# A mixture of 32 experts in 16 blocks of 128 slots and one for the overflow, or in 13 blocks ordered by token counts

## The chip, the core and the metric

One core of a Trainium2 chip runs the whole program. The metric is the device time of one execution in microseconds; the kernel before was run three times.

## The reference

Two transformer-like blocks run one after the other on 512 tokens of 1024 numbers, in float32. Only the expert layer that ends the first block changes:

```python
g_prob = softmax(t @ w_rg + b_rg)            # one of 4 groups
e_prob = softmax(e_logits of that group)     # top 2 of its 8 experts
for every expert e of 32:
    hid = silu(t @ w_gate[e]) * (t @ w_up[e]) * combine[:, e]
    y += hid @ w_down[e]                      # 1024 -> 256 -> 1024
```

So there are 1024 pairs of a token and an expert, and each expert has three matrices of 1024 x 256 floats, 100.7 MB in all, that come from HBM once per execution.

## The kernel before

A router stage gives each token its two experts, their weights (`Wc`) and its place in each expert's queue (`rank`). Each expert has `CAP` = 64 places. Two experts share a block of 128 slots, two blocks make a round of the loop at L1253, and there are eight rounds. For a round, `onehot` (L1055) builds tables token x slot: `ph` with ones, and `pw` with the combining weights, made on POOL (L1070). `gather_piece` (L1074) multiplies the tokens, kept as a high part `gh` and a low part `gl`, with `ph`, and so puts the round's 256 slots in columns (`xg`).

For a block, gate-up (L1270) multiplies the slots with the gate and up weights `we` of its two experts, each in 64 of the 128 output rows: one expert occupies columns 0 to 63 of the array, the other 64 to 127. `slots_back` (L1091) transposes the block's `pw` by four products (L1095). `hidden` (L1103) applies silu on ACT and DVE, `hidden_t` (L1110) transposes the result by two products (L1113), ACT copies it (L1116), and the down product (L1293) uses the weights `wd`. Outputs are split into two parts (`eoh`, `eol`, L181 and L184). `combine` (L1129; products L1125 and L1126) adds the slots of the round before into the tokens `x1`, eight chunks of 128 columns. The order on TensorE is written by hand: gate-up, transposes, four chunks of combining, hidden transposes, two gather pieces for the next round, down.

All weights are loaded through SP's queue, in program order. `load_up` (L1035) takes tiles of 512 KB from a ring of eight (`wp`), which a block's gate-up weights fill; `load_down` (L1048) takes halves of 256 KB from another ring of eight (`hp`). The second block's gate-up weights lie in spare buffers. A load waits in SP's queue until the last product that reads its tile is done, and the loads behind it wait with it.

Tokens past the 64th of an expert go to overflow blocks. The first of these, block 0, always runs: its expert's number is read from memory by SP (L1137), its weights are loaded a second time (L1141, L1146), its tokens are gathered at L1167, and its products are L1305 and L1318. Further overflow blocks run in a loop (L1348) as often as needed. The places of the overflow are worked out on DVE (L1200 to L1250). `last_ada` are modulation rows whose transposes (L348) stand in front of the first gate-up; their products (L334) come earlier, in four column groups of 32.

## Time and profile before

| | |
|---|---|
| median of three runs | 1312.29 us |
| runs | 1311.86, 1312.29, 1320.4 us |
| the profiled execution: span from the first to the last instruction | 1319.8 us |
| PE busy, share of the span | 1261.9 us, 96% |
| DVE, ACT, POOL busy | 764.8, 474.7, 274.3 us |
| bytes moved | 208.13 MB, mean 158 GB/s |

The profiled execution's own time is not among the runs by name; its span is 0.6 us below the slowest of them. PE's busy time includes pipelined products that overlap, and a busy PE is not PE at its peak. The expert stage lies between about 453 and 780 us of the span. Timelines give an instruction's start and length; products overlap, so their cost is read from one start to the next.

### The profile page before, as it was taken

Reading aid. Unit: us, or ns where it says so; the run is one execution under the profiler, and the core shown is the slowest. Engines: PE = TensorE matmul, PEld = TensorE weight load, DVE = VectorE, ACT = ScalarE, POOL = GpSimd, SP = SyncE. Lnnn points to the kernel's source line nnn. Section 1 sums busy time; section 2 is a strip of 40 time slices with the busy share of each in tenths; the row PEclk is TensorE's granted clock in tenths of the full one; section 3 lists DMA queues with packets and bytes.
Section 4 is the critical chain, followed back from the end, with each engine's and each line's share of the span. In section 5 each row is a group of like instructions: output and inputs, shape, how many; then the busy total and the mean of one; then the engine's idle time right before and its main releaser. Section 6 shows DMA issues by size and latency. Waiting matters only on the chain. (4 is left out here: it accounts for less than half of the span.)

```text
span 1319.8 us, 18564 instructions
## 1 busy us (share of the span) xinstructions
PE 1261.9 (96%) x6814; PEld 902.2 (68%) x6820; DVE 764.8 (58%) x1616; ACT 474.7 (36%) x1052; POOL 274.3 (21%) x239
## 2 busy tenths in 40 slices
PE   6999999999999799999999999999999999899997
PEld 3676766788887545655565458777777777676676
DVE  6857776544443723232333364477778777677767
ACT  4444445333333322212222223344444444345330
POOL 4243121000010210000000041223333330333321
PEclk9999999999999899999999969999999999989999
DMA  9625334122274468998899813122121122112221
GB/s 356 231 80 178 119 112 176 49 96 96 96 287 138 177 227 333 339 351 327 322 346 351 304 50 116 68 80 81 64 81 48 64 81 80 37 44 80 97 80 64
DMA packets 77341, 208.13 MB, mean 158 GB/s; under 512 B 9344, under 2 KB 9472, under 8 KB 77248
## 3 DMA queue, kind: packets, MB, share of 16 engines
q1 hardware_dynamic: 75264, 200.80, 42.2%
q0 software_dynamic: 1840, 6.03, 1.4%
q8 instruction: 55, 0.90, 0.3%
q14 instruction: 38, 0.31, 0.1%
q10 hardware_dynamic: 144, 0.09, 0.1%
HBM read 204.79 MB, written 2.10 MB: 157 GB/s over the span
## 5 line engine op out<-in xcount | busy, mean ns | idle before, releaser
L200 DVE TENSOR_TENSOR wlo<-w,whi 128x512 fp32r<-128x512 f32 x200 | 157.0, 824 | 114.0 <-ACT whi L199 101.6
L211 PE MATMUL ps_d<-x2h,whi 128*128 128x512 f32 x352 | 143.2, 407 | 0.0
L213 PE MATMUL ps_d<-x2h,wlo 128*128 128x512 f32 x352 | 138.4, 393 | 0.0
L212 PE MATMUL ps_d<-x2l,whi 128*128 128x512 f32 x352 | 138.1, 392 | 0.0
L199 ACT ACTIVATE whi<-w 128x512 fp32r<-128x512 f32 x200 | 115.4, 620 | 37.9 <-PE ps_d L212 16.5
L667 ACT ACTIVATE p<-st,mn 128x128 f32<-128x128 f32 (+3 forms) x128 | 71.0, 556 | 148.2 <-DVE mn L659 148.2
L1270 PE MATMUL ps_o<-we,xg 128*64 128x512 f32 x512 | 112.6, 592 | 0.0
L1270 PEld LDWEIGHTS ps_o<-we,xg 128*64 128x64 f32 x512 | 36.7, 137 | 72.7 <-issue 64.4
L184 DVE TENSOR_TENSOR eol<-ps_sc,eoh 128x512 fp32r<-128x512 f32 x33 | 22.8, 692 | 102.8 <-ACT eoh L181 94.5
L211 PEld LDWEIGHTS ps_d<-x2h,whi 128*128 128x128 f32 x352 | 66.8, 190 | 20.4 <-issue 5.3
L211 PE MATMUL ps_d<-h1h,whi 128*128 128x512 f32 x192 | 78.4, 409 | 0.0
L213 PEld LDWEIGHTS ps_d<-x2h,wlo 128*128 128x128 f32 x352 | 66.5, 189 | 15.3 <-DVE wlo L200 0.6
L212 PEld LDWEIGHTS ps_d<-x2l,whi 128*128 128x128 f32 x352 | 66.9, 190 | 12.5
L213 PE MATMUL ps_d<-h1h,wlo 128*128 128x512 f32 x192 | 75.0, 391 | 0.0
L212 PE MATMUL ps_d<-h1l,whi 128*128 128x512 f32 x192 | 74.9, 390 | 0.0
L1083 PE MATMUL ps_d<-ph,gh 128*128 128x256 f32 x256 | 66.1, 296 | 1.6 <-DVE ph L1062 1.6
L1070 POOL TENSOR_TENSOR pw<-ph,route 128x256 f32<-128x256 f32 x32 | 21.7, 707 | 218.6 <-PE ps_o L1270 199.1
L1084 PE MATMUL ps_d<-ph,gl 128*128 128x256 f32 x256 | 64.5, 290 | 0.0
L692 DVE TENSOR_SCALAR p<-p,rl 128x128 f32<-128x128 f32 (+3 forms) x128 | 58.7, 459 | 4.6
L1293 PE MATMUL ps_sc<-wd,p 128*64 128x512 f32 x256 | 58.5, 598 | 2.1 <-ACT p L1116 2.0
L1083 PEld LDWEIGHTS ps_d<-ph,gh 128*128 128x128 f32 x256 | 51.0, 199 | 2.1 <-ACT gh L939 1.3
L1084 PEld LDWEIGHTS ps_d<-ph,gl 128*128 128x128 f32 x256 | 51.1, 200 | 0.0
(669 smaller groups left out, 2756.5 us busy)
## 6 DMA issues: line engine op xcount, KB each, us to landing
we<-in_w_e_dram SPq DMA_DIRECT2D x124, 512.0 KB, 7.7
w<-in_w_dram SPq DMA_DIRECT2D x68, 512.0 KB, 3.3
wd<-in_w_e_dram SPq DMA_DIRECT2D x132, 256.0 KB, 4.7
wa<-in_w_ada_dram SPq DMA_DIRECT2D x32, 512.0 KB, 5.2
w<-in_w_out_dram SPq DMA_DIRECT2D x32, 512.0 KB, 3.2
wa<-in_w_ada_dram SPq DMA_DIRECT2D x32, 256.0 KB, 5.4
w<-in_v_dram SPq DMA_DIRECT2D x12, 512.0 KB, 7.5
w<-in_w_o_dram SPq DMA_DIRECT2D x8, 512.0 KB, 3.7
```

The costliest lines, as they stand in the source:

```text
L184: (ge if lo_eng == "g" else ve).tensor_tensor(lo, src, hi.bitcast(F32), op=OP.subtract)
L199: se.activation(hi, raw[:, s], AF.Copy)
L200: ve.tensor_tensor(lo, raw[:, s], hi.bitcast(F32), op=OP.subtract)
L211: pe.matmul(o, lh, rh, start=first, stop=False)
L212: pe.matmul(o, lh, rl, start=False, stop=False)
L213: pe.matmul(o, ll, rh, start=False, stop=last)
L667: se.activation(pt[:, :w], u["st"][s][:, :w], AF.Exp, bias=u["mn"][s], scale=-1.0, accum_out=l)
L692: ve.tensor_scalar(u["p"][s][:, :w], u["p"][s][:, :w], rl, None, op0=OP.mult)
L1083: pe.matmul(o[:, q * 256:(q + 1) * 256], gh[g][:, s], r, start=t == 0, stop=False)
L1084: pe.matmul(o[:, q * 256:(q + 1) * 256], gl[g][:, s], r, start=False, stop=t == 3)
L1270: pe.matmul(gu[64 * s:64 * s + 64, :], xg[k // 2][:, c0:c0 + CAP], ws[j, s, k // 2][k % 2], start=k == 0, stop=k == KC - 1, tile_position= ...
L1293: pe.matmul(o[64 * s:64 * s + 64, :], ht[:, kk * P + 64 * s:kk * P + 64 * s + 64], ws[j, s, kk, h], start=kk == 0, stop=kk == 1, tile_posi ...
```

## The change

The 32 experts are put into 13 blocks of four quarters of 32 slots. Experts 0 to 5 keep two quarters each (64 places), in blocks 0 to 2, and their loads need no number from the chip. The other 26 are sorted on the chip by their token counts: the largest gets three quarters (96 places), the next twelve two, the last thirteen one (32). Blocks 3, 6 and 9 hold two experts of 64 places; blocks 4, 5, 7, 8, 10 and 11 hold one of 64 and two of 32; block 12 holds the one of 96 and one of 32. Blocks go in groups of two, the last group of three. Block 0 for the overflow is gone: tokens without a place go to the loop, which starts from its first pass.

The sort: DVE counts for each expert how many have more tokens (`place`) and builds a selecting table `pick` from it and a new constant table, which POOL's queue loads (`rtab`). Two transposes and four small products then give, for each quarter, the places and weights of the tokens (`zkeys`, `zwts`) and its expert's number (`eid`). SP reads these numbers into registers ahead of the loads of block 3 and later ones. A third expert's weights lie in the small rings `tab` and `pt`.

The order on TensorE is new too. Two chunks of combining and a gather piece stand between the quarters of gate-up; two more chunks stand behind the slot transposes; the rest comes behind the hidden transposes. The last block opens three chunks of the final combining ahead of its down product. The modulation transposes and the overflow's arithmetic are moved behind block 0's gate-up.

```diff
+NS = 6
+TILES = [2] * NS + [3] + [2] * 12 + [1] * 13
+GROUPS = ((0, 1), (2, 3), (4, 5), (6, 7), (8, 9), (10, 11, 12))
+def _blocks():
+    two, one = list(range(NS + 1, NS + 13)), list(range(NS + 13, NE))
+    out = [[(2 * i, 2), (2 * i + 1, 2)] for i in range(NS // 2)]
+    for _ in range(3):
+        out.append([(two.pop(0), 2), (two.pop(0), 2)])
+        for _ in range(2):
+            out.append([(two.pop(0), 2), (one.pop(0), 1), (one.pop(0), 1)])
+    out.append([(NS, 3), (one.pop(0), 1)])
+    assert not two and not one
+    return out
+BLOCKS = _blocks()
+ZT = [(p, 32 * i) for b in BLOCKS[2:] for p, n in b for i in range(n)]
+NZ = len(ZT)
...
+    def expert(p):
+        if p < NS:
+            return p
+        z = [q for q, _ in ZT].index(p)
+        return nc.values_load(eid[0:1, z:z + 1], engines=[mybir.EngineType.SP], min_val=0, max_val=NE - 1)
+    def fetch(t, e, i, c=slice(0, 1024)):
+        if isinstance(e, int):
+            nc.sync.dma_start(t, w_e[e, i, :, c])
+        else:
+            nc.sync.dma_start(t, w_e[bass.ds(e, 1), i, :, c].rearrange("o p c -> p (o c)"))
+    def halves(alloc, e, i):
+        t = [alloc() for h in range(2)]
+        for h in range(2):
+            fetch(t[h], e, i, slice(h * 512, (h + 1) * 512))
+        return t
+    regs = {}
+    def load_up(n, spare=False):
+        regs[n] = [expert(p) for p, _ in BLOCKS[n]]
         for i in range(4):
-            for s in range(2):
+            for s, e in enumerate(regs[n]):
                 if spare:
-                    t = [big("we") for h in range(2)]
-                    for h in range(2):
-                        nc.sync.dma_start(t[h], w_e[2 * j + s, i, :, h * 512:(h + 1) * 512])
+                    ws[n, s, i] = halves(lambda: big("we"), e, i)
+                elif s == 2 and i < 2:
+                    ws[n, s, i] = halves(lambda: tmp("tab"), e, i)
                 else:
-                    t = wload(w_e[2 * j + s, i], "we")
-                    t = [t[:, 0:512], t[:, 512:1024]]
-                ws[j, s, i] = t
-    def load_down(j):
-        for h in range(2):
-            for i in range(2):
-                for s in range(2):
-                    t = ws[j, s, i, h] = hp.tile([P, 512], F32, tag="h", name="wd")
-                    nc.sync.dma_start(t, w_e[2 * j + s, 4 + i, :, h * 512:(h + 1) * 512])
+                    t = wp.tile([P, 1024], F32, tag="w", name="we")
+                    fetch(t, e, i)
+                    ws[n, s, i] = [t[:, 0:512], t[:, 512:1024]]
+    def load_down(n):
+        es = regs.pop(n)
+        for ss in ((0, 1), (2,)):
+            for h in range(2):
+                for i in range(2):
+                    for s in ss:
+                        if s < len(es):
+                            t = hp.tile([P, 512], F32, tag="h", name="wd") if s < 2 else tmp("pt")
+                            ws[n, s, 4 + i, h] = t
+                            fetch(t, es[s], 4 + i, slice(h * 512, (h + 1) * 512))
...
         o = bank("d")
-        for q in range(2):
-            d = 2 * c + q
+        w = ph[0].shape[1]
+        n = 512 // w
+        for q in range(n):
+            d = n * c + q
             for t in range(4):
                 g = 2 * t + d // 4
                 s = slice((d % 4) * P, (d % 4 + 1) * P)
-                r = ph[t // 2][:, (t % 2) * 256:(t % 2 + 1) * 256]
-                pe.matmul(o[:, q * 256:(q + 1) * 256], gh[g][:, s], r, start=t == 0, stop=False)
-                pe.matmul(o[:, q * 256:(q + 1) * 256], gl[g][:, s], r, start=False, stop=t == 3)
+                pe.matmul(o[:, q * w:(q + 1) * w], gh[g][:, s], ph[t], start=t == 0, stop=False)
+                pe.matmul(o[:, q * w:(q + 1) * w], gl[g][:, s], ph[t], start=False, stop=t == 3)
         x_ = big("xg")
-        for q in range(2):
-            s = slice(q * 256, (q + 1) * 256)
-            se.activation(x_[:, s], o[:, s], AF.Identity, bias=mods[:, 24 + 2 * c + q:25 + 2 * c + q])
-        xg.append(x_)
+        for q in range(n):
+            s = slice(q * w, (q + 1) * w)
+            se.activation(x_[:, s], o[:, s], AF.Identity, bias=mods[:, 24 + n * c + q:25 + n * c + q])
+            xg.append(x_[:, s])
...
-    def load_block0():
-        er = nc.values_load(eb0[0:1, 0:1], engines=[mybir.EngineType.SP], min_val=0, max_val=NE - 1)
...
+    rtab = big("rtab")
+    ge.dma_start(rtab[:, :288], consts_d[:, 640:928])
+    ph, pw = onehot(rank[:, :, 0:4], Wc[:, :, 0:4], CAP, weights)
...
-    run(last_ada[0][1], last_ada[1][1])
...
+    keyr, keyc, own, place = cv(NE), cv(1), cv(NE), cv(1)
+    ve.scalar_tensor_tensor(keyr, cnt, float(NE), rtab[:, 220:252], op0=OP.mult, op1=OP.add)
+    ve.tensor_tensor(own, keyr, rtab[:, 253:285], op=OP.mult)
+    ve.tensor_reduce(keyc, own, axis=AX.X, op=OP.add)
+    above = cv(NE)
+    ve.tensor_scalar(above, keyr, keyc, None, op0=OP.is_gt)
+    ve.tensor_reduce(place, above, axis=AX.X, op=OP.add)
+    pick = big("pick")
+    ve.tensor_scalar(pick[:, :4 * NZ], rtab[:, :4 * NZ], place, None, op0=OP.is_equal)
...
+    o = bank("tr")
+    pe.transpose(o[:, 0:P], rank1.rearrange("p t e -> p (t e)"), ident)
+    pe.transpose(o[:, P:2 * P], Wc.rearrange("p t e -> p (t e)"), ident)
+    turned = big("turned")
+    ve.tensor_copy(turned[:, :2 * P], o[:, :2 * P])
+    zkeys, zwts = cz(4, NZ), cz(4, NZ)
+    eid = small([P, NZ], "eid", I32, bufs=1)
...
+    def order_out():
+        o = bank("tr")
+        for i in range(2):
+            pe.matmul(o[:, 4 * NZ * i:4 * NZ * (i + 1)], turned[:, i * P:(i + 1) * P], pick[:, :4 * NZ], start=True,
+                      stop=True)
+        pe.matmul(o[:, 8 * NZ:9 * NZ], rtab[:, 252:253].to_broadcast([P, P]), pick[:, :NZ], start=True, stop=True)
+        pe.matmul(o[:, 9 * NZ:9 * NZ + NE], capc[:, 0:1].to_broadcast([P, P]), ident[:, :NE], start=True, stop=True)
+        v = lambda a: a.rearrange("p (t z) -> p t z", t=4)
+        ve.tensor_copy(eid, o[:, 8 * NZ:9 * NZ])
+        ve.tensor_tensor(zkeys, v(o[:, :4 * NZ]), rtab[:, None, 176:176 + NZ].to_broadcast([P, 4, NZ]), op=OP.subtract)
+        ve.tensor_copy(zwts, v(o[:, 4 * NZ:8 * NZ]))
+        ve.tensor_copy(caps, o[:, 9 * NZ:9 * NZ + NE])
+    def spill_in():
...
+    def gate_up(n, b, i, gu, xg):
+        whole = all(c == 2 for _, c in BLOCKS[n])
+        for k in (2 * i, 2 * i + 1):
+            z = 0
+            for s, (_, c) in enumerate(BLOCKS[n]):
+                m = 64 if whole else 32
+                for z in range(z, z + c, m // 32):
+                    a = 32 * z
+                    pe.matmul(gu[a:a + m, :], xg[k][:, b * P + a:b * P + a + m], ws[n, s, i][k % 2], start=k == 0,
+                              stop=k == KC - 1, tile_position=(0, a))
+                z += m // 32
...
     prev = None
-    for q in range(NQ):
-        if q + 1 < NQ:
-            ph, pw_next = onehot(q + 1)
+    opened = []
+    for gi, group in enumerate(GROUPS):
+        nxt = GROUPS[gi + 1] if gi + 1 < len(GROUPS) else ()
         xg_next, outs, pts = [], [], []
-        for b in range(2):
-            j = 2 * q + b
-            if j + 2 < NE // 2:
-                if j:
-                    load_up(j + 2)
-                load_down(j + 2)
-            elif q == NQ - 1 and b == 0:
-                w0 = load_block0()
-                po0, pw0 = onehot0()
+        nb = len(group)
+        gathers = list(range(2 * len(nxt) if len(nxt) < 3 else 8))
+        gathers = [gathers] if gi == 0 else [gathers[i * len(gathers) // nb:(i + 1) * len(gathers) // nb] for i in range(nb)]
+        for b, n in enumerate(group):
+            if n + 2 < len(BLOCKS):
+                if n:
+                    load_up(n + 2)
+                load_down(n + 2)
+            sums = list(range(8 * b // nb, 8 * (b + 1) // nb)) if prev else []
+            if gi:
+                todo = gathers[b]
+            else:
+                todo = gathers[0] if b else []
+            if nxt and (b == 1 if gi == 0 else b == 0):
+                z0 = 4 * (nxt[0] - 2)
+                ph, pw_next = onehot(zkeys[:, :, z0:z0 + 4 * len(nxt)], zwts[:, :, z0:z0 + 4 * len(nxt)], 32)
+            def fillers(c, g):
+                for _ in range(c):
+                    if sums:
+                        combine(*prev, sums.pop(0))
+                for _ in range(g):
+                    if todo:
+                        gather_piece(ph, todo.pop(0), xg_next)
             gu = bank("o")
-            for k in range(KC):
-                for s in range(2):
-                    c0 = (k % 2) * 256 + (2 * b + s) * CAP
-                    pe.matmul(gu[64 * s:64 * s + 64, :], xg[k // 2][:, c0:c0 + CAP],
-                              ws[j, s, k // 2][k % 2], start=k == 0, stop=k == KC - 1,
-                              tile_position=(0, 64 * s))
-            pt, csh = slots_back([pw[t // 2][:, (t % 2) * 256 + b * P:(t % 2) * 256 + (b + 1) * P] for t in range(4)])
+            few = not nxt
+            g2 = 2 if len(nxt) == 3 else 1
+            gate_up(n, b, 0, gu, xg)
+            fillers(0 if few else 1, 0)
+            gate_up(n, b, 1, gu, xg)
+            fillers(0 if few else 1, 0)
+            gate_up(n, b, 2, gu, xg)
+            fillers(0, g2)
+            gate_up(n, b, 3, gu, xg)
+            pt, csh = slots_back([w[:, b * P:(b + 1) * P] for w in pw])
             hd = hidden(gu, csh, P)
-            if prev:
-                for m in range(4 * b, 4 * b + 4):
-                    combine(*prev, m)
-                ht = hidden_t(hd, P)
-            if q + 1 < NQ:
-                for c in range(2 * b, 2 * b + 2):
-                    gather_piece(ph, c, xg_next)
-                if not prev:
-                    ht = hidden_t(hd, P)
-            elif b == 0:
-                xs0 = gather0(po0)
-            else:
-                xo = turn0(xs0)
-            po = []
-            for h in range(2):
-                o = bank("sc")
-                for kk in range(2):
-                    for s in range(2):
-                        pe.matmul(o[64 * s:64 * s + 64, :], ht[:, kk * P + 64 * s:kk * P + 64 * s + 64],
-                                  ws[j, s, kk, h], start=kk == 0, stop=kk == 1,
-                                  tile_position=(0, 64 * s))
-                po.append(split(o, "eo", "s", "v"))
-            outs.append(po)
+            if gi == 0 and b == 0:
+                order_out()
+                run(last_ada[0][1], last_ada[1][1])
+                spill_in()
+            fillers(2, 0 if gi else 2 * g2)
+            if not nxt and b == nb - 1:
+                opened.append(combine_open(outs, pts, 0))
+            ht = hidden_t(hd, P)
+            fillers(8, 8)
+            if not nxt and b == nb - 1:
+                opened += [combine_open(outs, pts, m) for m in (1, 2)]
+            outs.append(down(n, ht))
             pts.append(pt)
         prev = (outs, pts)
-        xg, pw = xg_next, pw_next
...
+    outs, pts = prev
     for m in range(8):
-        o = op_[m] if m < 3 else combine_open(*prev, m)
-        combine_open([(eo, eo)], [pt], m, o, True, slice(64 * (m // 4), 64 * (m // 4) + 64))
+        o = opened[m] if m < len(opened) else combine_open(outs[:-1], pts[:-1], m)
+        combine_open(outs[-1:], pts[-1:], m, o, True)
         add_x(o, m)
```

On PE, a block of the kernel before, from the down product of the block ahead (`ps_o` is gate-up's bank, `ps_sc` down's; an instruction may stand for two on the chip):

```order
L1293 MATMUL ps_sc<-wd,p 64x512 x8
L1270 MATMUL ps_o<-we,xg 64x512 x16
L1095 MATMUL ps_tr<-cst,pw 128x128 x4
L1125 MATMUL ps_d<-pt__4905,eoh 128x512
L1126 MATMUL ps_d<-pt__4905,eol 128x512
```

And block 4 of the change, the first with three experts, from the same place:

```order
L1317 MATMUL ps_sc<-wd,p 64x512 x8
L1302 MATMUL ps_o<-we,xg 32x512 x3
L1302 MATMUL ps_o<-tab,xg 32x512
L1302 MATMUL ps_o<-we,xg 32x512 x3
L1302 MATMUL ps_o<-tab,xg 32x512
L1182 MATMUL ps_d<-pt__5026,eoh 128x512
L1183 MATMUL ps_d<-pt__5026,eol 128x512
L1182 MATMUL ps_d<-pt__5229,eoh 128x512
L1183 MATMUL ps_d<-pt__5229,eol 128x512
L1302 MATMUL ps_o<-we,xg 32x512 x3
```

Sixteen products of 64 columns became 32 of 32 columns, and combining moved in between the quarters.

On SP, the loads of the kernel before (the second and third block):

```order
L1042 DMA we<-in_w_e_dram 128x512 x16
L189 DMA we<-in_w_e_dram 128x1024 x8
L1053 DMA wd<-in_w_e_dram 128x512 x16
L189 DMA we<-in_w_e_dram 128x1024 x8
L1053 DMA wd<-in_w_e_dram 128x512 x8
```

And the start of block 4's in the change, behind the last of its three number reads:

```order
L1064 TENSOR_LOAD eid
L1064 ISA x2
L1070 ISA
L1070 DMA we<-in_w_e_dram 128x1024
L1070 ISA
L1070 DMA we<-in_w_e_dram 128x1024
L1070 ISA
L1070 DMA tab<-in_w_e_dram 128x512
```

Each load has a register instruction in front of it now, and the third expert's first tiles go to another ring.

## Rows read from the trace of the kernel before

**Rows 1.** The page, part 2: busy tenths of DMA and its rate, 40 slices.

```profile
DMA  9625334122274468998899813122121122112221
GB/s 356 231 80 178 119 112 176 49 96 96 96 287 138 177 227 333 339 351 327 322 346 351 304 50 116 68 80 81 64 81 48 64 81 80 37 44 80 97 80 64
```

**Rows 2.** Windows: stretch, length, busy us (count) of PE, PEld, DVE, ACT, POOL, clock, DMA.

```profile
453.56:755.64 302.08, 299.19 (x1615) 168.38 (x1614) 107.65 (x227) 66.39 (x159) 19.42 (x28) 1.00 0.86 319
...
494.20:719.30 225.10, 225.10 (x1227) 129.87 (x1226) 78.11 (x148) 50.62 (x120) 13.93 (x20) 1.00 0.91 337
```

**Rows 3.** Timeline, PE, one block: start us, us, line, op, out<-in, shape, count.

```profile
543.10 7.04 PE L1270 MATMUL ps_o<-we,xg 128*64 128x512 f32 x32
550.07 0.66 PE L1095 MATMUL ps_tr<-cst,pw 128*128 128x128 f32 x4
550.49 0.48 PE L1125 MATMUL ps_d<-pt__4905,eoh 128*128 128x512 f32 x1
...
554.24 0.38 PE L1113 MATMUL ps_tr<-cst,p 128*128 128x128 f32 x2
554.37 0.36 PE L1083 MATMUL ps_d<-ph,gh 128*128 128x256 f32 x1
...
558.17 0.28 PE L1084 MATMUL ps_d<-ph,gl 128*128 128x256 f32 x1
558.38 3.65 PE L1293 MATMUL ps_sc<-wd,p 128*64 128x512 f32 x16
561.86 7.04 PE L1270 MATMUL ps_o<-we,xg 128*64 128x512 f32 x32
```

**Rows 4.** Timeline, PE, start and end of the expert stage.

```profile
452.60 1.03 PE L348 MATMUL ps_d<-cst,sq 128*128 128x128 f32 x8
453.56 7.09 PE L1270 MATMUL ps_o<-we,xg 128*64 128x512 f32 x32
...
753.70 1.94 PE L1318 MATMUL ps_sc<-wd,p 128*64 128x512 f32 x8 [0.43 <-ACT p L1116]
756.36 0.50 PE L1125 MATMUL ps_d<-pt__6995,eoh 64*128 64x512 f32 x1 [0.72 <-ACT eoh L181]
...
773.26 0.62 PE L1126 MATMUL ps_sc<-pt__6995,eol 64*128 64x512 f32 x1
...
779.88 0.50 PE L211 MATMUL ps_sc<-whi,x2h 128*128 128x512 f32 x1
```

**Rows 5.** Timeline, PE, a modulation row in four column groups.

```profile
429.75 3.64 PE L334 MATMUL ps_d<-wa,crep 128*32 128x512 f32 x32
```

**Rows 6.** Timeline, all engines: end of the hidden chain, copy of its transposes.

```profile
552.68 0.48 DVE L1107 SCALAR_TENSOR_TENSOR p<-sq,csh,ps_o 128x256 f32<-128x256 f32 x1
...
554.71 0.39 ACT L1116 ACTIVATE p<-ps_tr 128x256 f32<-128x256 f32 x1 [2.98 <-PE ps_tr L1113]
```

**Rows 7.** Windows of 2 and 4 us, in this and other stages.

```profile
8.00:12.00 4.00, 2.67 (x14) 0.62 (x12) 0.29 (x2) 1.12 (x2) 0.55 (x1) 1.00 1.05 388
376.00:380.00 4.00, 4.00 (x19) 3.30 (x19) 2.26 (x3) 1.67 (x3) 2.90 (x5) 1.00 1.05 390
540.00:542.00 2.00, 2.00 (x12) 0.72 (x10) 0.00 (x0) 0.94 (x3) 0.00 (x0) 1.00 0.21 56
554.00:556.00 2.00, 2.00 (x17) 1.90 (x16) 1.79 (x3) 0.39 (x1) 0.00 (x0) 1.00 1.03 416
764.00:768.00 4.00, 4.00 (x8) 2.15 (x8) 1.13 (x2) 0.00 (x0) 0.00 (x0) 0.50 0.00 0
```

**Rows 8.** Timeline of SP, loads with an expert number from a register.

```profile
732.91 2.31 SPq L1141 DMA_DIRECT2D we<-in_w_e_dram  x4
```

**Rows 9.** Source line L1137, the number itself: duration in ns, min/median/max.

```profile
L1137 SPq TENSOR_LOAD <-oeb x1: 483/483/483, 731.9 to 731.9; - x1
```

**Rows 10.** Timeline, PE, after its wait for the router.

```profile
440.39 0.21 PE L1011 MATMUL ps_tr<-Ab,trib 128*128 128x32 bf16 x1 [7.00 <-DVE Ab L1004]
...
445.06 0.41 PE L1084 MATMUL ps_d<-ph,gl 128*128 128x256 f32 x1
```

More of the change, by code (lines that the diff above doesn't have):

```diff
@@ new lines, in down @@
+    def down(n, ht):
+        whole = all(c == 2 for _, c in BLOCKS[n])
+        po = []
+        for h in range(2):
+            o = bank("sc")
+            for kk in range(2):
+                z = 0
+                for s, (_, c) in enumerate(BLOCKS[n]):
+                    m = 64 if whole else 32
+                    for z in range(z, z + c, m // 32):
+                        a = 32 * z
+                        pe.matmul(o[a:a + m, :], ht[:, kk * P + a:kk * P + a + m], ws[n, s, 4 + kk, h], start=kk == 0,
+                                  stop=kk == 1, tile_position=(0, a))
+                    z += m // 32
+            po.append(split(o, "eo", "s", "v"))
+        return po
@@ L1857, in _tables @@
     cst[:, 4, 64:72] = 8 - np.arange(8)
+    pick = np.full((P, 288), 0, np.float32)
+    z = np.array([p for p, _ in ZT], np.float32)
+    for t in range(4):
+        pick[:, t * NZ:(t + 1) * NZ] = np.where(i[:, None] // NE == t, z[None, :], np.float32(-1000))
+    pick[:, 176:176 + NZ] = [1 + r for _, r in ZT]
+    first = lambda e: NE - 1 - e + 1e6 * np.maximum(NS - e, 0)
+    pick[:, 220:252] = first(np.arange(NE))
+    pick[:, 252] = i % NE
+    pick[i, 253 + i % NE] = 1
     q, c = i[:, None], np.arange(512)[None, :]
```

172 lines of the change are left out of this document (58 added, 114 removed).

## The prediction

> **What bounds the kernel now.** The page's slices come first [rows 1]: in one long run of slices, the 16th to the 23rd, the DMA engines are nearly full (8 and 9 tenths, 304 to 351 GB/s). That is the expert stage, which the change rewrites. The table by stretch [rows 2] says how full: from 494.2 to 719.3 PE is busy for all of its 225.10 us at a granted clock of 1.00, and the DMA share is 0.91 at 337 GB/s. So TensorE is the bound, and the transfers follow close behind. One block read in order [rows 3] gives the price list: gate-up 543.10 to 550.07, 6.97 us; four transposes 0.42; sixteen combining products 3.75; two transposes 0.13; thirty-two gather products 4.01; the down product 3.48. Together 18.76 us for 128 slots, sixteen times over. The ends of the stage [rows 4] show a first gate-up at 453.56, behind the two modulation transposes at 452.60 (0.96 us), and a 17th, half-size block for the overflow, whose down product ends at 753.70 + 1.94 = 755.64. Then 36 combining products run from 756.36 to 773.88, and the next stage's first product starts at 779.88, 24.2 us after that last down product.
>
> **What TensorE has to do afterwards.** Thirteen blocks, six of them whole (two experts with 64 places) and seven of quarters of 32 columns.
> - Gate-up of a whole block 6.97 us. The mixed ones issue 64 instructions instead of 32. The only present product in four column groups of 32, with the same 512 moving columns, is the modulation row [rows 5]: 32 instructions in 3.64 us, 0.114 us each, so 7.28 us. Six of the one and seven of the other: 92.8 us. Down: 6 x 3.48 + 7 x 32 x 0.114 = 46.4 us.
> - Gathers: four groups of 64 products at 4.01/32 = 0.125 us, 32.1 us; the last with 384 columns, between 0.125 and the 0.234 us of a 512-column product (3.75/16), say 0.18, 11.5 us.
> - Combining: ten blocks in front of the last down product, 37.5 us, and twelve products opened early, 2.8 us. Transposes: 13 x 0.55 = 7.2 us. The sort's four small products and the moved modulation transposes: 1.9 us.
> - A new wait. Today 3.75 us of combining stand between slot transposes and hidden transposes; now two sums, 1.88 us, because the others moved between the quarters of gate-up. The hidden chain ends at 553.16, 2.67 us after the slot transposes' end at 550.49 [rows 6], so PE waits 0.8 us a block. Block 0 and the first of the last group also have nothing behind the hidden transposes, whose copy ends 0.86 us after they start [rows 6]. About 11 us in all.
> - Gate-up is now interrupted by sums and gathers. A step between unlike products shows in [rows 3]: the last gather product starts at 558.17 and the first down product at 558.38, 0.21 us later, where gather products follow at 0.125. Six such steps a block are 0.5 us, 6 us in all.
>
> Sum: 92.8 + 46.4 + 43.6 + 40.3 + 7.2 + 1.9 + 11 + 6 = 249 us from 452.8 (the modulation transposes leave, two sort transposes come): TensorE alone would end the last down product at 702.
>
> **What the transfers need.** The 32 experts weigh what they did, 3.146 MB each (three matrices of 1024 x 256 floats); only the overflow expert's second copy, 3.1 MB, goes. Six mixed blocks now need three experts, 9.44 MB, for 18.9 us of products. What rate is to be had when the queue never starves? The rows with a share above 1.0 [rows 7] say 388 and 390 GB/s in two other stages and 416 in the middle of a block; the stage's 337 at share 0.91 extends to 370. I take 385: a little under the two stretches of 388 and 390, which hold a full share for 4 us, not for 2. At that rate a three-expert block is 24.5 us, a two-expert block 16.3 us: the bound changes sides in the mixed blocks.
>
> The Trainium skill ("DMA: Bandwidth & Descriptors", section Specifications) gives one core about 358 GB/s of HBM; the rows above say more was moved here, so the measurement decides, and that figure comes back only as a rival.
>
> By order of events: block 0 takes 14.6 us (6.97 + 0.42 + 1.9 + 0.8 + 0.13 + 0.86 + 3.48), block 1 19.0 (its four gathers inside), block 2 20.1, so gate-up of block 3 starts near 506.5. One ring of eight tiles holds one block's gate-up weights, so block 4's can only be fetched as block 3's quarters finish, from about 509. Blocks 4 to 12 are 6 x 9.44 + 3 x 6.29 = 75.5 MB: 196 us, to 705. In the whole blocks 6 and 9 PE needs 20.1 us for 16.3 us of transfer, and the ring can't run ahead: some 3 us of idle queue each, 711. Behind the last byte stands what PE has not done: the last quarter's weights land 2.1 MB (5.5 us) earlier, and from there a quarter of gate-up, transposes, sums, the opened products and down are 11.6 us, so 6 us: **the last down product ends at 717 instead of 755.6, 38.7 us earlier.**
>
> SP's queue: a load with an expert number from a register took 2.31/4 = 0.58 us to issue and the number itself 0.48 [rows 8, 9]; 26 loads and three numbers are 17 us of a 24.5 us block, hidden by the transfers; were it more than 24.5, mixed blocks would go at SP's pace. The sort on DVE runs beside gathers and gate-up 0, and the one new table load stands on POOL's queue ahead of the first weighted one-hot tables, which nobody wants before the slot transposes of block 0; the spill arithmetic, now behind block 0's hidden chain, is beside down 0 and gate-up 1. Should it delay the second group's one-hot tables, that is 1 to 2 us at block 1, within the range. The tail keeps its 36 products, so 24.2 us again.
>
> **The rivals.**
> 1. *Transfers stay at the rate of now.* If 0.91 is what this ring permits, 75.5 MB at 337 GB/s take 224 us, 28 us more: 1302. For it: the ring stays one block deep and waits on PE. Against: in [rows 7] the same queue shows 416 GB/s, and today's shortfall is a gap once a block in which PE still holds the tiles (56 GB/s from 540 to 542). By the Trainium skill's 358 GB/s it would be 211 us, 1289. Chance 0.17.
> 2. *Slower: the clock falls in the starved blocks.* TensorE would wait about 5 us in each of six blocks. After a wait of 7.00 us the profile shows matmuls at half clock [rows 10], 0.41 us for a gather product that takes 0.28 in [rows 3], and from 764 to 768 it grants 0.50 although PE is busy throughout [rows 7]: 1.2 instead of 2.4 GHz. A block's 18.9 us at half clock are 37.8, against 24.5 of transfer: 13 us more, six times, 80 us: 1354. It decides from where the half clock covers 0.3 of a block's work (18.9 x 1.3 = 24.5); from 0.75 on, six blocks cost 52 us, the gain and 13 us more. Against: 8 to 12 us shows PE busy 2.67 of 4.00 us at clock 1.00, and the waits here come in pieces of 1 to 2.5 us between quarters. "TensorE: Matmul & The Clock Gate" of the Trainium skill, section Loop structure matters more than you think, warns of just this: a wait for a transfer ahead of each batch of matmuls lets the clock drop. The trace agrees in the 7.00 us case, and not in the one of 8 to 12 us. Chance 0.05 in full, 0.09 for a part of it (1285 to 1310).
> 3. *It doesn't do what it says: tokens spill.* Counting the reference's router on its drawn inputs, experts hold 9 to 71 tokens; without the first six, the largest has 71 (of 96), the 13th 32 (of 64), the 14th 31 (of 32). No pass of the overflow loop, then. A pass would fetch 3.1 MB with nothing beside it, 8 us, and run its products in series: two whole blocks' time, 38 us, as a bound, or 1312 for one and more for others. Chance 0.03.
>
> **How the numbers follow.** The profile's span of 1319.8 us lies 0.6 below the slowest of the three runs (1320.4) and 7.5 above their median of 1312.29. The half-clock tail is worth about 9 us (17.5 us for 36 products that cost 8.4 at 0.234), so the median may be a run without it; the saving is the same if both have the same tail. 1312.3 - 38.7 = **1274**, chance 0.64. Its own range is 1258 to 1285: at 416 GB/s the transfers end level with TensorE's 702, 15 us less; a tail with the other clock is 9 us either way. For 8 in 10 it has to take in most of rival 1: 1258 to 1301. About 1 per cent, 13 us, is what a measurement of this kernel can tell from no change. Faster by more: 0.64 + 0.14 + 0.05 = 0.83. Within: the slow end of rivals 1 and 2 and a single spill pass, 0.10. Slower: 0.07.
>
> **What would show it.** Right: a last down product near 717 us; whole blocks 2 and 3 about 20 us apart, mixed ones 24 to 25; a DMA share of 1.0 and 380 GB/s or more from 510 on; PE waits for `we`, `tab` and `wd` loads of 20 to 25 us in total; mixed gate-up rows of 0.114 us. Wrong: a share that stays at 0.9 with PE waiting (rival 1); granted clock at 0.5 inside mixed blocks (rival 2); loads on the overflow loop's lines (rival 3); or PE rows in mixed blocks that take twice the modulation row's time, which would put TensorE back in front.

## The result, and the profile after

The changed kernel takes 1280.41 us (median of four runs, 1279.1 to 1283.8), the kernel before 1313.63 beside it; the ratio is 0.974, with an interval of 0.9706 to 0.9775. The forecast was 1274 within 1258 to 1301. The profiled execution has a span of 1279.3 us; its own time is 1281.25.

The two profiles differ by 40.5 us of span, the medians by 33.2. In the profiles 31.4 us lie ahead of the last down product, which ends at 724.28 instead of 755.64 [rows 4]. Another 9.4 lie behind it, up to the next stage: the 36 closing products took 17.5 us before, most of it at half clock [rows 4, 7], and take 8.4 us at full clock now. Runs of before come at 1310 to 1315 or at 1320 to 1323 us, and every profiled execution of it was one of the latter.

The page of the change, part 2, answers to [rows 1]:

```profile
PEclk9999999999999899999999999999999999999999
DMA  9624345032264656899999733222221212112321
GB/s 353 243 85 149 129 135 187 29 114 91 93 221 156 219 198 243 317 390 388 386 357 396 291 99 99 68 81 69 78 70 50 83 67 73 43 34 86 113 66 66
```

In the 18th to the 22nd slice the transfers are at 357 to 396 GB/s, where they were at 322 to 351, and TensorE's clock is at 9 tenths in every slice but the 14th, which lies ahead of the expert stage. The table by stretch answers to [rows 2, 7] (columns as there):

```profile
453.43:724.28 270.85, 259.72 (x1548) 123.26 (x1547) 82.59 (x169) 51.18 (x119) 14.91 (x20) 1.00 0.92 347
511.90:528.40 16.50, 15.94 (x88) 8.68 (x84) 4.32 (x8) 3.63 (x9) 0.00 (x0) 1.00 0.93 354
528.40:532.00 3.60, 3.60 (x26) 1.25 (x28) 2.58 (x5) 0.60 (x1) 1.39 (x3) 1.00 0.15 27
544.00:656.00 112.00, 108.67 (x676) 54.86 (x675) 34.72 (x60) 22.48 (x51) 6.66 (x8) 1.00 1.02 387
656.00:668.00 12.00, 11.94 (x82) 4.50 (x80) 1.38 (x2) 2.36 (x4) 0.00 (x0) 1.00 0.89 336
668.00:712.40 44.40, 39.67 (x224) 12.08 (x224) 9.28 (x17) 5.08 (x12) 0.00 (x0) 1.00 1.03 393
511.90:712.40 200.50, 191.24 (x1170) 87.45 (x1166) 56.12 (x98) 35.95 (x82) 9.39 (x12) 1.00 0.99 374
724.28:732.66 8.38, 8.38 (x36) 6.61 (x36) 5.58 (x8) 1.64 (x3) 0.00 (x0) 1.00 0.34 112
```

The first row is the stage, from the first gate-up to the last down product: 270.85 us, where it was 302.08. From 544 to 656 and from 668 to 712.4 the DMA share is above 1.0 at 387 and 393 GB/s. The third row is a hole, a stretch in which the queue moves next to nothing: 3.6 us at 27 GB/s. The last row is the closing sums.

On TensorE, the rows that answer to [rows 3, 4]: the down products of blocks 1 and 2, the start of the whole block 3 and of the mixed block 4, the last block, the next stage.

```profile
483.88 3.65 PE L1317 MATMUL ps_sc<-wd,p 128*64 128x512 f32 x16
...
504.46 3.65 PE L1317 MATMUL ps_sc<-wd,p 128*64 128x512 f32 x16
507.95 1.89 PE L1302 MATMUL ps_o<-we,xg 128*64 128x512 f32 x8
...
528.65 0.63 PE L1302 MATMUL ps_o<-we,xg 128*32 128x512 f32 x3
534.61 1.92 PE L1302 MATMUL ps_o<-we,xg 128*32 128x512 f32 x16
...
703.61 3.53 PE L1302 MATMUL ps_o<-we,xg 128*32 128x512 f32 x22 [0.28 <-DMA we<-in_w_e_dram]
707.36 2.34 PE L1302 MATMUL ps_o<-we,xg 128*32 128x512 f32 x16 [0.22 <-DMA we<-in_w_e_dram]
709.91 2.35 PE L1302 MATMUL ps_o<-we,xg 128*32 128x512 f32 x16 [0.21 <-DMA we<-in_w_e_dram]
712.48 1.90 PE L1302 MATMUL ps_o<-we,xg 128*32 128x512 f32 x10 [0.22 <-DMA we<-in_w_e_dram]
...
720.64 3.64 PE L1317 MATMUL ps_sc<-wd,p 128*32 128x512 f32 x32
...
739.08 0.50 PE L235 MATMUL ps_sc<-whi,x2h 128*128 128x512 f32 x1
```

A whole block takes 528.65 - 507.95 = 20.70 us, the forecast said 20.1. A quarter of mixed gate-up is sixteen products that begin some 0.11 us apart, as the modulation row's did [rows 5]. In the last block every quarter starts behind a load, and behind the last of them (712.48) 11.80 us of work remain; the forecast said 11.6. The closing stretch, from the end of the last down product to the next stage, is 14.8 us instead of 24.2. On SP's queue, the loads of blocks 3 and 4 (start, time spent issuing, line, tile, count):

```profile
505.57 4.35 SPq L1070 DMA_DIRECT2D wd<-in_w_e_dram  x8
511.91 0.91 SPq L1070 DMA_DIRECT2D we<-in_w_e_dram  x2
513.03 0.87 SPq L1070 DMA_DIRECT2D tab<-in_w_e_dram  x2
514.16 1.48 SPq L1070 DMA_DIRECT2D we<-in_w_e_dram  x2
515.84 1.18 SPq L1070 DMA_DIRECT2D tab<-in_w_e_dram  x2
517.63 13.87 SPq L1070 DMA_DIRECT2D we<-in_w_e_dram  x6
531.73 4.55 SPq L1070 DMA_DIRECT2D wd<-in_w_e_dram  x8
```

Block 3's down weights are issued from 505.57 on, behind block 2's down product (504.46); block 4's loads follow them and three number reads, at 511.91. The six loads at 517.63 take 13.87 us. Of block 4's ten gate-up tiles from the ring of eight, the last two need tiles that hold block 4's own first quarter, which starts at 528.65. The wait of SP's queue stands in the trace (from 516 to 533; us in total, times, longest):

```profile
SPq L1070 <- PE ps_o L1302: 9.5, 2, 9.2
```

That is the hole.

### The profile page after: what moved, and what is told of

It reads as the page before. It is cut to its first block, busy times and chain, and to the rows that moved or that the text cites. A ratio compares the mean times of both kernels' runs of the same rounds, so it can differ in the third digit from the quotient of the medians.

```text
span 1279.3 us, 18709 instructions
## 1 busy us (share of the span) xinstructions
PE 1213.9 (95%) x6746; PEld 854.1 (67%) x6746; DVE 740.4 (58%) x1566; ACT 459.0 (36%) x1011; POOL 271.0 (21%) x232
## 5 line engine op out<-in xcount | busy, mean ns | idle before, releaser
L1302 PE MATMUL ps_o<-we,xg 128*32 128x512 f32 (+1 forms) x592 | 111.0, 600 | 3.1 <-DMA we<-in_w_e_dram 2.8
L1302 PEld LDWEIGHTS ps_o<-we,xg 128*32 128x32 f32 (+1 forms) x592 | 26.5, 117 | 67.0 <-issue 40.2
L1145 ACT ACTIVATE xg<-ps_d,mods 128x256 f32<-128x256 f32 (+1 forms) x48 | 21.4, 489 | 108.8 <-PE ps_d L1141 108.8
L1140 PE MATMUL ps_d<-ph,gh 128*128 128x256 f32 (+1 forms) x192 | 54.0, 311 | 1.2 <-DVE ph L1114 1.2
L208 DVE TENSOR_TENSOR eol<-ps_sc,eoh 128x512 fp32r<-128x512 f32 x26 | 17.9, 691 | 59.6 <-ACT eoh L205 59.6
L1141 PE MATMUL ps_d<-ph,gl 128*128 128x256 f32 (+1 forms) x192 | 52.0, 300 | 0.0
L1124 POOL TENSOR_TENSOR pw<-ph,route 128x256 f32<-128x256 f32 (+1 forms) x24 | 17.2, 746 | 162.7 <-PE ps_o L1302 95.2
L1317 PE MATMUL ps_sc<-wd,p 128*32 128x512 f32 (+1 forms) x272 | 47.6, 597 | 1.1 <-ACT p L1173 1.1
L703 PEld LDWEIGHTS ps_tr<-cst,p 128*128 128x128 f32 x320 | 38.0, 140 | 14.4 <-issue 4.2
```

The source lines that it names most:

```text
L703: pe.transpose(tr[:, j * P:(j + 1) * P], u["p"][s][:, j * P:(j + 1) * P], ident)
L1140: pe.matmul(o[:, q * w:(q + 1) * w], gh[g][:, s], ph[t], start=t == 0, stop=False)
L1141: pe.matmul(o[:, q * w:(q + 1) * w], gl[g][:, s], ph[t], start=False, stop=t == 3)
L1302: pe.matmul(gu[a:a + m, :], xg[k][:, b * P + a:b * P + a + m], ws[n, s, i][k % 2], start=k == 0, stop=k == KC - 1, tile_position=(0, a))
L1317: pe.matmul(o[a:a + m, :], ht[:, kk * P + a:kk * P + a + m], ws[n, s, 4 + kk, h], start=kk == 0, stop=kk == 1, tile_position=(0, a))
```

## The experiments

The theory: from block 4 on the transfers set the end, and TensorE waits for weights. The rivals: TensorE's own work in the finer order sets it; SP's pace does. First gate-ups begin between 450.2 and 454.1 us in the profiles, for reasons ahead of the stage, so stage lengths are compared. The kernel before has 302.08 or 302.09 us in all three profiles and the change 270.85 and 271.49, so a difference of some 0.6 us says nothing:

| kernel | median us | ratio to before (interval) | stage, us |
|---|---|---|---|
| before | 1313.63 | | 302.08 |
| the change | 1280.41 | 0.974 (0.9706 to 0.9775) | 270.85 |
| third expert not loaded | 1256.88 | 0.9554 (0.951 to 0.9597) | 249.87 |
| fixed numbers | 1278.01 | 0.9716 (0.9672 to 0.976) | 271.39 |
| fill behind gate-up | 1276.92 | 0.9708 (0.9662 to 0.9753) | 269.93 |
| other order of blocks | 1274.22 | 0.9691 (0.9647 to 0.9735) | 265.47 |
| before without block 0 | 1297.5 | 0.9858 (0.981 to 0.9905) | 289.58 |
| other order, early third expert | 1273.5 | 0.9669 (0.9623 to 0.9716) | 265.74 |
| last tiles later | 1277.03 | 0.9697 (0.9649 to 0.9745) | 267.46 |
| order, early third, last tiles | 1272.04 | 0.9661 (0.9634 to 0.9689) | 263.50 |
| order, last tiles | 1270.7 | 0.9659 (0.9632 to 0.9687) | 262.77 |
| the change again | 1281.6 | 0.9737 (0.971 to 0.9763) | 271.49 |

### Are the transfers the bound? The third expert's weights are not loaded

```diff
-            for s, e in enumerate(regs[n]):
+            for s, e in enumerate(regs[n][:2]):
...
+            if len(regs[n]) == 3:
+                ws[n, 2, i] = ws[n, 1, i]
...
-        for ss in ((0, 1), (2,)):
+        for ss in ((0, 1),):
...
+                    if len(es) == 3:
+                        ws[n, 2, 4 + i, h] = ws[n, 1, 4 + i, h]
```

> Leaves out the weights of the third expert of each mixed block: its products read the tiles of the second, so 18.9 MB fewer are moved and TensorE's work stays. If the transfers set the end (theory), TensorE's waits for weights, 20.7 us by the profile of the change, go: last down product at 703 to 706 instead of 724.3, span 1258 to 1262. If TensorE's own work in the mixed blocks sets it (rival: small products and many steps), span within 4 us of 1279.3.

The stage and a mixed block of the last group in this kernel:

```profile
452.01:701.88 249.87, 242.25 (x1548) 120.29 (x1547) 82.58 (x169) 51.17 (x119) 14.91 (x20) 1.00 0.83 301
```

```profile
669.25 7.05 PE L1306 MATMUL ps_o<-we,xg 128*32 128x512 f32 x64
698.24 3.64 PE L1321 MATMUL ps_sc<-wd,p 128*32 128x512 f32 x32
```

249.87 us, 21.0 less than the change, with the same 1548 products on TensorE (first row of the change's stretches). The last down product ends at 701.88, just ahead of the 703 to 706 expected; 1.4 us of that is an earlier first gate-up. So TensorE's work was foreseen to a microsecond (249), and 21.0 us of the change's stage are waits for transfers. The rival on TensorE's work falls. With two experts a block also needs only eight tiles of the ring, so this run takes out the holes together with the bytes and cannot tell them apart; the run with the last tiles loaded later, below, takes out the larger hole alone.

### SP's pace: fixed expert numbers

```diff
-        if p < NS:
+        if p < NE:
             return p
```

> The loads of all blocks take expert numbers fixed in the program (the sort still gives places and weights, so the weights loaded are not those of the sorted experts). Bytes and products stay; the number reads and the register instruction ahead of each load go. If the transfers set the end, 0 to 3 us earlier than 1279.3. If the pace of SP's queue sets it (rival: 0.58 us a load and 0.5 to 0.7 a number), 10 us earlier or more.

The stage is 271.39 us, the change's within the difference of its two profiles, and the ratio is the same within the intervals. A number read takes SP about 0.27 us in the change, less than the 0.48 of [rows 9]:

```profile
L1064 SPq TENSOR_LOAD <-eid x26: 262/272/478, 488.7 to 697.3; - x26
```

The reads and register instructions are hidden behind the transfers. That rival falls too.

### The order of the filling work

```diff
-            gate_up(n, b, 0, gu, xg)
-            fillers(0 if few else 1, 0)
-            gate_up(n, b, 1, gu, xg)
-            fillers(0 if few else 1, 0)
-            gate_up(n, b, 2, gu, xg)
-            fillers(0, g2)
-            gate_up(n, b, 3, gu, xg)
+            for i in range(4):
+                gate_up(n, b, i, gu, xg)
...
-            fillers(2, 0 if gi else 2 * g2)
+            fillers(8 if gi else 0, 0 if gi else 3 * g2)
```

> Sums and gather pieces stand behind the slot transposes again, gate-up's quarters follow each other directly. If the transfers set the end, the 0.56 us waits for the hidden chain (10 of them) go and come back as waits for weights, because the quarters want them earlier: span 1276 to 1285. If TensorE's own order costs the time, 5.6 us of those waits and about 0.2 us for each of the steps between unlike products go: 1268 to 1272.

Two down products of whole blocks that follow each other, in this kernel:

```profile
480.33 3.65 PE L1317 MATMUL ps_sc<-wd,p 128*64 128x512 f32 x16
...
499.09 3.65 PE L1317 MATMUL ps_sc<-wd,p 128*64 128x512 f32 x16
```

They are 18.76 us apart, exactly a block's price before [rows 3]; in the change, 20.58 (483.88 to 504.46). So work between the quarters, with the wait for the hidden chain that it brings, costs TensorE 1.8 us a block (the forecast said 0.8 + 0.5). The stage is only 0.9 us shorter, hardly more than the change's two profiles differ, because the time comes back as waits. TensorE's weight loads waited for `we` tiles, in the change and then here (us in total, times, longest):

```profile
PEld ps_o L1302 <- DMA we<-in_w_e_dram: 18.0, 20, 1.2
```

```profile
PEld ps_o L1302 <- DMA we<-in_w_e_dram: 35.2, 37, 2.5
```

The span of 1274.7 looks like a gain of 4.6, but 3.2 of that is a first gate-up at 450.22.

### Does the order of blocks matter?

```diff
-    for _ in range(3):
-        out.append([(two.pop(0), 2), (two.pop(0), 2)])
-        for _ in range(2):
-            out.append([(two.pop(0), 2), (one.pop(0), 1), (one.pop(0), 1)])
-    out.append([(NS, 3), (one.pop(0), 1)])
+    for kind in "MEMWMWMMWM":
+        if kind == "W":
+            out.append([(two.pop(0), 2), (two.pop(0), 2)])
+        elif kind == "M":
+            out.append([(two.pop(0), 2), (one.pop(0), 1), (one.pop(0), 1)])
+        else:
+            out.append([(NS, 3), (one.pop(0), 1)])
```

> Same 13 blocks, other order: places 3 to 12 are mixed, the block of 96 and 32, mixed, whole, mixed, whole, mixed, mixed, whole, mixed. Same products and bytes. If the transfers set the end, their holes at 528 to 532 and 660 to 668 fill, since the heavy blocks begin at place 3 while TensorE is still ahead: last down product 3 to 8 us earlier, span 1271 to 1276. If TensorE's work sets it, the sum is the same in any order: 1279 plus or minus 2.

This kernel by stretch, the stage and the twelve microseconds from 500:

```profile
450.96:716.43 265.47, 255.22 (x1548) 122.74 (x1547) 82.55 (x169) 51.11 (x119) 14.90 (x20) 1.00 0.93 348
500.00:512.00 12.00, 12.00 (x79) 5.27 (x80) 3.47 (x6) 2.42 (x5) 0.00 (x0) 1.00 0.58 222
```

The stage is 265.47 us, 5.4 less, with the same products and bytes. It depends on when the heavy blocks come, as transfers would have it. A hole stands from 500 to 512, at a share of 0.58.

### Where does the hole come from? The last two tiles loaded later

```diff
+                    if len(regs[n]) == 3 and i == 3 and s:
+                        late.append((t, e, i))
+                    else:
                         fetch(t, e, i)
...
+                        if down_loads == 6:
+                            while late:
+                                fetch(*late.pop(0))
+                        down_loads += 1
```

> The change's own order of blocks; in mixed blocks the last two gate-up loads, which wait for the block's own first quarter (ten tiles in a ring of eight), stand behind six of the down loads instead of ahead of all. If the hole of 528 to 532 in the transfers is made by that wait, it closes and those of 656 to 668 too: 3 to 4 us less, first gate-up to last down product 267 to 268 us against 270.9. If the hole has another cause, no change; if the last tiles come too late for the fourth quarter, 1 to 3 us more.

The stretch around the start of block 4's gate-up (526.94 here), and three from block 11:

```profile
526.70:530.30 3.60, 3.60 (x26) 1.25 (x28) 2.59 (x5) 0.60 (x1) 1.39 (x3) 1.00 0.93 311
686.00:688.00 2.00, 0.00 (x0) 0.00 (x0) 0.00 (x0) 0.00 (x0) 0.00 (x0) 0.90 1.06 411
690.00:692.00 2.00, 2.00 (x9) 0.55 (x9) 0.00 (x0) 0.00 (x0) 0.00 (x0) 0.50 1.05 387
694.00:696.00 2.00, 2.00 (x10) 1.47 (x10) 0.15 (x1) 0.94 (x3) 0.00 (x0) 0.89 1.02 407
```

The hole is closed (311 GB/s instead of 27), so it was the wait for the ring. The stage is 267.46, 3.4 less, in spite of a new cost. In block 11 the first of the two moved tiles comes late, and TensorE stands for 4.29 us:

```profile
682.87 2.34 PE L1311 MATMUL ps_o<-we,xg 128*32 128x512 f32 x14 [0.23 <-DMA we<-in_w_e_dram]
689.50 4.91 PE L1311 MATMUL ps_o<-we,xg 128*32 128x512 f32 x12 [4.29 <-DMA we<-in_w_e_dram]
```

During that wait, from 685.2 to 689.5, the clock falls to 0.50, 1.2 GHz, and stays there until past 694; twelve products take 4.91 us, where in the change's last block sixteen take 2.35, waits inside the row included in both. This is rival 2's mechanism, once.

One part of the expectation failed: the dip that the change has from 656 to 668, ahead of block 10, did not close. In this run's trace it stands from 656 to 660, and around it (645 to 670) SP's queue waits for something else:

```profile
656.00:660.00 4.00, 4.00 (x28) 1.12 (x28) 1.38 (x2) 1.19 (x2) 0.00 (x0) 1.00 0.67 203
```

```profile
SPq L1070 <- PE ps_sc L1326: 6.8, 3, 6.1
```

With the two tiles out of the way, block 10's down loads wait 6.1 us for block 9's down product, which frees their ring. So this dip belongs to the whole block 9, in which the loads catch up with TensorE, and of the change's two only the one at block 4 is shown to be the ten tiles' work.

### An early third expert

```diff
+    def load_third(n):
+        regs[n] = [expert(p) for p, _ in BLOCKS[n]]
+        for i in range(2):
+            ws[n, 2, i] = halves(lambda: tmp("tab"), regs[n][2], i)
+        for h in range(2):
+            for i in range(2):
+                t = ws[n, 2, 4 + i, h] = tmp("pt")
+                fetch(t, regs[n][2], 4 + i, slice(h * 512, (h + 1) * 512))
...
+                if n == 1:
+                    load_third(3)
+                    load_down(2)
                 if n:
                     load_up(n + 2)
-                load_down(n + 2)
+                    load_down(n + 2)
```

> The order of blocks of the experiment before it (mixed block at place 3), and eight tiles of block 3's third expert (2.1 MB) are loaded ahead of block 2's down weights, which wait for block 1's down product; the queue is idle there. If the transfers set the end, 2.1 MB less in the full stretch at 390 GB/s is 5.4 us: first gate-up to last down product 260 to 262 us against 265.5, span about 1267. If that idle queue is of no use (the stretch from 490 on is not full from its start), within 1.5 us of 265.5.

This kernel by stretch:

```profile
464.00:484.00 20.00, 20.00 (x124) 11.91 (x122) 8.46 (x31) 5.78 (x14) 2.76 (x4) 1.00 0.74 264
500.00:512.00 12.00, 11.44 (x74) 5.12 (x73) 4.22 (x7) 2.42 (x5) 0.00 (x0) 1.00 0.38 137
```

A miss: the 2.1 MB do come early, and the stage is 265.74, against 265.47 without them. Only the hole of 500 to 512 grew, from a share of 0.58 to 0.38. The expectation had counted bytes as if they could be saved up. The next two runs tell whether the hole alone is to blame. Both move the last two tiles at places 3, 5, 7 and 9 behind six down loads; the first has the early third expert as well.

```diff
+                    if len(regs[n]) == 3 and i == 3 and s and n in (3, 5, 7, 9):
+                        late.append((t, e, i))
+                    else:
                         fetch(t, e, i)
...
```

> Other order of blocks, block 3's third expert early, and for the mixed blocks at places 3, 5, 7 and 9 the last two gate-up loads behind six down loads (not for the mixed blocks further on, where the queue has no hole and such a load came 4.3 us late). Early tiles alone gave nothing, and a hole of 500 to 512 (share 0.38) stood in their place: there the queue waits on block 3's last two tiles. If that is the cause, the hole closes now and the 2.1 MB count: first gate-up to last down product 260 to 262 us against 265.5, span 1267 to 1269. If the early tiles are worth nothing for another reason, the same as the run beside it without them.

> The same without the early third expert: other order of blocks and the later last tiles at places 3, 5, 7 and 9. The hole of 500 to 512 (share 0.58 with the order alone) closes in part: 2 to 3 us under 265.5, 262 to 264, span 1269 to 1271. If the transfers have no hole that the ring of eight makes, 265 to 266.

From 500 on, with the early third expert and the later last tiles:

```profile
500.00:512.00 12.00, 12.00 (x78) 5.46 (x82) 3.47 (x6) 2.42 (x5) 0.00 (x0) 1.00 0.71 240
512.00:650.00 138.00, 134.04 (x881) 69.82 (x874) 45.30 (x79) 29.08 (x67) 9.38 (x12) 1.00 0.98 368
```

and without the early third expert, behind the row of the whole stage:

```profile
451.16:713.93 262.77, 252.36 (x1548) 121.17 (x1547) 82.59 (x169) 51.18 (x119) 14.90 (x20) 1.00 0.94 352
464.00:484.00 20.00, 20.00 (x124) 11.92 (x122) 7.65 (x28) 6.18 (x15) 2.76 (x4) 1.00 0.40 143
500.00:512.00 12.00, 12.00 (x78) 5.45 (x82) 3.48 (x6) 2.42 (x5) 0.00 (x0) 1.00 0.99 328
512.00:650.00 138.00, 134.04 (x881) 69.83 (x874) 45.30 (x79) 29.09 (x67) 9.38 (x12) 1.00 1.00 378
```

The first run is a miss, 263.50 us where 260 to 262 were expected; the second came as expected, at 262.77. The hole closes without the early tiles (0.99). With them it does not quite (0.71), and from 512 to 650 the rate is 368 GB/s instead of 378: what was moved early is moved slower later. The gate-ups at places 4 to 10 start at the same times in both traces, 526.35 to 653.82, for the most part at TensorE's own pace. So bytes moved ahead of a ring that holds one block bought nothing; that the ring's depth is the reason is argued, a deeper one was not tried. Without them the kernel is the fastest of all: 1270.7 us against 1281.6 for the change beside it. Its stage is 262.77, still 12.9 above TensorE alone; the last three blocks, which have no gathers, take from 653.82 to 713.93, 60.1 us, where they take 47.2 (in the change's order) without the third expert's loads.

> The change itself once more beside the two, for a comparison on the same chip: 1279 to 1284 us, first gate-up to last down product 270 to 272 us.

As expected, 1281.6 us and a stage of 271.49.

### What leaving out block 0 gives

```diff
-            elif q == NQ - 1 and b == 0:
-                w0 = load_block0()
-                po0, pw0 = onehot0()
...
-            elif b == 0:
-                xs0 = gather0(po0)
-            else:
-                xo = turn0(xs0)
...
-        o = op_[m] if m < 3 else combine_open(*prev, m)
-        combine_open([(eo, eo)], [pt], m, o, True, slice(64 * (m // 4), 64 * (m // 4) + 64))
-        add_x(o, m)
+        combine(*prev, m)
```

> The kernel before without the overflow block that always runs: its weights are not loaded and the tokens past the 64th place of one expert are dropped. If the gain of the change comes from 13 blocks in place of 16, this alone gives little: block 15's down product ended some 14 to 15 us ahead of block 0's, but the closing sums stay, so 1297 to 1301 against 1312. If the overflow block is most of the 33 us, 1280 to 1285.

1297.5 us, as the first case said, and a stage (to block 15's down product here) 12.5 us shorter than before's. So of the change's 31.2 us of stage, some 12.5 are block 0's and, by difference, 18.7 come from the thirteen blocks.

### The half-clock tail of the kernel before

> The kernel before once more, for a second profile of it. The prediction put the median of before 7.5 us under its first profile and gave as a possible reason that the 36 closing products ran at half clock only in some executions. If so, a run near 1311 us shows them in about 8.4 us at granted clock 1.00 and the same last down product as the first profile, about 302 us after the first gate-up. If the 7.5 us lie elsewhere, the closing products take 17.5 us again or the stretch from first gate-up to last down product differs by several us.

> The kernel before a third time, since both profiled executions so far (1320.4 and 1321.88 us) had the half-clock closing products, and others of its runs lie at 1310 to 1315. If this one comes out there, the profile should show the 36 closing products at clock 1.00 in about 8.4 us, the next stage's first product about 15 us after the last down product (24.2 now), and first gate-up to last down product at 302 us as before. If it comes out at 1320 to 1323, the tail is at half clock again.

They came out at 1321.88 and 1319.74 us, and the granted clock behind the last down product (754.06 in the second) is this:

```profile
756.00:760.00 4.00, 4.00 (x11) 2.11 (x11) 2.35 (x4) 0.00 (x0) 0.00 (x0) 0.67 0.59 184
760.00:764.00 4.00, 4.00 (x9) 2.31 (x9) 1.21 (x2) 0.00 (x0) 0.00 (x0) 0.50 0.01 2
```

Half clock again. The stage is 302.09 us in both, as in the first profile (302.08), so the 7.5 us between the first profile and the median do not lie in it. That the runs near 1312 lack the half clock fits the 9 us between the two sets of times, but no such run was profiled, so it stays open. What comes ahead of the sums differs: in [rows 4] TensorE waits 0.43 us for the last down product and 0.72 for the first sum, and in the change's last block it has no wait behind 712.48. In every profile of the change and of its variants the 36 sums take 8.4 us at a clock of 1.00. Whether those waits set off the half clock is not shown.

## Why the prediction was right, and where it was off

**What bounds it.** Right: without 18.9 MB of loads the same products take 21.0 us less. Mixed blocks were forecast 24 to 25 us apart. By the starts of the down products, blocks 5 and 8, each the second mixed one of its pair, take 23.1 and 25.1 us and blocks 4 and 7, the first ones, 20.7, which is a whole block's time.

**TensorE's work.** Right in the sum: 249 us forecast, 249.87 measured without the third expert's loads. That it fits to a microsecond is partly luck. Mixed gate-up was cheaper (7.05 us for 64 products, forecast 7.28; 1.6 us for seven blocks), work between the quarters dearer (1.8 us a block, forecast 1.3; 5 us for ten), and the rest of the difference lies in terms that were not compared one by one.

**The transfers' rate.** Right: 385 GB/s taken, 387 to 393 measured at a full share, so rival 1's 337 falls. The 358 GB/s that the Trainium skill gives ("DMA: Bandwidth & Descriptors", Specifications) is passed here in two stretches of 112 and 44 us.

**The transfers' start and amount: the step that was mis-sized.** The last quarter's weights were forecast to land at 711 - 5.5 = 705.5; TensorE takes them at 712.48, 7.0 us later, and that is nearly all of the 7.3 us by which the last down product missed 717. The sum began with block 4's loads at 509. The first of them went out at 511.91, 2.9 us later. Half of that is TensorE's: block 3's gate-up starts at 507.95 instead of 506.5. The other half is SP's queue, which had block 3's down loads ahead, 2.1 MB that could not be issued before block 2's down product, and then three number reads. From there to 712.4 the row by stretch gives 200.5 us x 374 GB/s = 75.0 MB, where the forecast had 75.5 - 2.1 = 73.4 up to the last quarter: 1.6 MB or 4 us more. Part of it was left over from block 3's down weights, of which some 1.5 of 2.1 MB had moved by 511.91 (6.34 us x 238 GB/s):

```profile
505.57:511.91 6.34, 6.34 (x30) 2.26 (x28) 2.13 (x3) 1.19 (x2) 0.00 (x0) 1.00 0.75 238
```

The other 1.0 MB is probably block 12's own down weights, issued from 703.62 on and under way before the last gate-up tile had landed; that is argued, not shown. At 390 GB/s throughout, 75.0 MB would take 192.3 us, so holes and slower stretches cost 8.2 us, where 6 were forecast; the better rate gives 2.4 back (73.4 MB at 390 instead of 385).

**Where the holes are.** Wrong in place, and partly in reason. They were put into the whole blocks 6 and 9. The larger one stands ahead of block 4, because a mixed block needs ten tiles of a ring of eight; the prediction had the ring, and not the ten. The one ahead of block 10 is near the place that was forecast, behind the whole block 9, and it stays when the ten tiles are taken out of the way, as the reason given (a ring that cannot run ahead of a whole block) would have it. At block 6 there is none: the share is 1.02 from 544 to 656.

**SP, the sort, the moved work.** Right: fixed numbers change nothing, so SP's reads are hidden. No run leaves out the sort or the moved work; blocks 0 to 2, where they stand, end 1.5 us later than forecast in all (507.95 against 506.5), which bounds what they cost TensorE beyond the forecast.

**The closing tail.** It was forecast at 24.2 us as before; it is 14.8, with the sums at full clock. In the profiles that is a gain of 9.4 that was not forecast. In the medians it does not show: 31.4 us of earlier last down product, 33.2 us of median. That the two profiles differ by 40.5 us, close to the 38.7 forecast, is luck: the tail makes up there for what the stage fell short.

**The rivals.** The clock stayed at 1.00 in the change's stage (rival 2), where weight loads waited at most 1.3 us at a time and TensorE itself stood still for at most 0.4 us behind a load. With the fill behind gate-up it stood still for up to 1.6 us, still at 1.00; the run with a 4.29 us wait shows that the mechanism is real. The Trainium skill ("TensorE: Matmul & The Clock Gate", Loop structure matters more than you think) warns of a long wait for a transfer ahead of every matmul; the run with 4.29 us agrees, and the change's short waits do not put it to the test. No instruction of the overflow loop ran (rival 3).

## What to carry to other kernels

When fewer, fuller blocks cut the compute and the bytes stay, work out the time of each engine and of the transfers from the first load that can still move, and put in what is already queued ahead of it. Count the tiles that a block wants against the ring that holds them: one tile too many makes the queue wait for the very block it feeds. Where the buffers hold one block, try other orders of heavy and light blocks: here another order of the same blocks gave 5.4 us, and closing the hole in it 2.7 more. Do not count on bytes saved up ahead of such a buffer: here 2.1 MB moved early bought nothing.

## What the runs showed of the hardware

- One queue held 387 to 393 GB/s for 112 and 44 us on one core, at a DMA share of 1.02 to 1.03. A share near 1.0 does not fix the rate: 328, 378 and 387 GB/s stand beside 0.99, 1.00 and 1.02.
- TensorE stood still behind a load for up to 1.6 us at a clock of 1.00 (fill behind gate-up); in a wait of 4.29 us behind several shorter ones (last tiles later) the clock fell, and it stood at 0.50 for some 7 us.
- In the kernel before, most of the closing products ran at half clock in all three profiled executions, although TensorE was busy throughout; in the change, its variants and the kernel without block 0 they did not. What set it off is not known.
